# First projection of a hybrid decoder layer: x in 256-column pieces and k-tiles turned two at a time

## The chip, the cores and the metric

The kernel runs on one core of one Trainium2 chip. The metric is the device time of one execution in microseconds (us); the median of three executions stands for a kernel. The other numbers come from one profiled execution of the same program: engine PE is TensorE (PEld its weight load), DVE is VectorE, ACT is ScalarE, POOL is GpSimd, and SP is the engine whose queue issues most of the DMAs. A letter q behind an engine's name means its instruction queue rather than its arithmetic.

## The reference, cut to what matters

One decoder layer over 256 tokens of width 2048, in float32:

```
h    = rms_norm(x, pre_norm_w)                  # x: 256 x 2048
proj = h @ w_in                                 # w_in: 2048 x 12304, cut into q, k, v, z, b, a of branch A
                                                # and q, k, v, z of branch B, and two gates
A    = gated DeltaNet(causal conv + SiLU of q, k, v; beta, g)  -> @ w_branch_a
B    = block-sparse attention(q, k, v)          -> @ w_branch_b
y    = (sigmoid(gate_a) * A + sigmoid(gate_b) * B) @ w_out
out  = x + rms_norm(y, post_norm_w)
```

The change concerns the first stage alone: x is loaded and transposed, and the first 512 of the 1024 key columns of branch A are computed, that is a 256 x 2048 by 2048 x 512 product.

## The kernel before

**Arithmetic.** A float32 operand is cut in two: `hi`, rounded to the matmul's input type, and `lo`, the rest. A product is hi x hi + hi x lo + lo x hi. For one k-tile (128 of the 2048 rows of the weight) the first stage has in SBUF a raw weight tile of 128 x 512 (`rawk`, shown as `rawf_k`), its two parts `hi_k` and `lo_k`, and the matching 128 columns of x, transposed and multiplied by `pre_norm_w`, as `hT[:, k]`: 256 columns of hi and 256 of lo. Four output blocks (`pfirst`, shown as `a_k`) stay in PSUM over all 16 k-tiles. Each k-tile takes four matmuls of `hi_k` with all 512 columns of `hT` and four of `lo_k` with its first 256 columns (`first_products`).

**Where the parts come from.** `turn(c)` transposes k-tiles of x on PE into PSUM (`hTp`; two k-tiles share one PSUM tile, two transposes each). `turned(...)` takes them out: ACT writes the hi half of `hT` (L253, with the norm's weight as scale), then DVE writes the lo half (L256). `first_split(k, 2)` cuts two raw weight tiles at once: ACT casts the hi part (L278, 128x1024), DVE subtracts (L279). `stats(c)` squares and sums 512 columns of x for the norm, one token tile on ACT (L266), the other on DVE (L269).

**Order.** All these instructions are held in the order in which the program writes them on each engine (`pin`); an engine takes its own strictly in that order. The first stage goes by four chunks `c` of 512 columns. SP issues two pieces of x (128 x 512 each) and then four weight tiles for each chunk; the small DMA of `pre_norm_w` (`nrow`) is the first on SP. In chunk c, PE does two k-tiles, then the eight transposes of chunk c + 1, then the other two k-tiles. The weight splits run ahead: when chunk c + 1 is turned (from the second chunk on), the tiles up to 4c + 5 have been split already, and the tiles 4c + 6 to 4c + 9 are split after the chunk's last two k-tiles. The buffers of the weight parts hold three pairs.

**What follows.** After k-tile 15, the sums of squares give `rstd` (a table load and a Sqrt on ACT, L316; small steps on DVE, L315 to L326), PE spreads it (`prr`, L327), and the next projection (`zg`) starts. From there on weights come in larger pieces through `wraw` and `split` (L225, L226).

The rule by which the chunk loop works before:

```
for c in range(NCH):
    first_products(parts[4 * c : 4 * c + 2])
    if c + 1 < NCH:
        turned(turn(c + 1))
    ...
    stats(c)
    first_products(parts[4 * c + 2 : 4 * c + 4])
    for k in (4 * c + 6, 4 * c + 8): ...  parts += first_split(k, 2)
```

Of the kernel before, what the change touches and what calls it, by code (L numbers as in the profile page):

```python
# [15 lines left out]
P = 128  # L16
# [58 lines left out]
def hybrid_layer(  # L75
# [15 lines left out]
    nc = tc.nc  # L91
    B, S, D = x.shape
    NT = S // P
    KT = D // P
# [29 lines left out]
    def acc_tile(name):  # L124
        return acc.tile([P, 512], F32, tag="acc", name=name)

    def aux_tile(name):
        return aux.tile([P, 512], F32, tag="aux", name=name)
# [17 lines left out]
    def mm(*args, **kwargs):  # L146
        return pin(nc.tensor.matmul(*args, **kwargs))  # L147

    def tr(*args):
        return pin(nc.tensor.transpose(*args))  # L150
# [8 lines left out]

    NCH = KT // 4  # L160
    nrow = cst.tile([KT, P], F32, name="nrow")
    nc.sync.dma_start(nrow, pre_norm_w.rearrange("o (k p) -> (o k) p", p=P))
    prow = big.tile([P, P], F32, tag="ga", name="prow")
    xall = big.tile([P, NT, D], F32, tag="u1", name="x")
    xs = [xall[:, t, :] for t in range(NT)]
    rawk = [big.tile([P, KT // 2, 512], F32, tag=f"g{i}", name=f"rawf_k{i}") for i in range(2)]
    for c in range(NCH):
        for t in range(NT):
            cs = slice(c * 512, (c + 1) * 512)
            nc.sync.dma_start(xs[t][:, cs], xf[t * P : (t + 1) * P, cs])  # L170
        for k in range(4 * c, 4 * c + 4):
            nc.sync.dma_start(rawk[k // 8][:, k % 8], w_in[k * P : (k + 1) * P, CK : CK + 512])


# [62 lines left out]
    def turn(c):  # L237

        pts = []
        for k in range(4 * c, 4 * c + 4):  # L240
            if k % 2 == 0:
                pt = aux_tile(f"hTp_{k}")
            pts.append((k, pt[:, k % 2 * S : (k % 2 + 1) * S]))
            for t in range(NT):
                tr(pts[-1][1][:, t * P : (t + 1) * P], xs[t][:, k * P : (k + 1) * P], ident)
        return pts

    def turned(pts):
        for k, pr in pts:
            if k == 1:  # L250
                pin(nc.vector.tensor_scalar_mul(hT[:, k, :S], pr, ncol[:, k : k + 1]))
            else:
                pin(nc.scalar.activation(hT[:, k, :S], pr, AF.Copy, scale=ncol[:, k : k + 1]))  # L253
        for k, pr in pts:
            pin(
                nc.vector.scalar_tensor_tensor(  # L256
                    hT[:, k, S:], pr, ncol[:, k : k + 1], hT[:, k, :S].bitcast(F32), op0=ALU.mult, op1=ALU.subtract
                )
            )

    def stats(c):
        cs = slice(c * 512, (c + 1) * 512)
        for t in range(NT):
            j0 = wk.tile([P, 512], BF16, tag="jy", name=f"jx_{c}_{t}")
            if t == 0:
                pin(nc.scalar.activation(j0, xs[t][:, cs], AF.Square, accum_out=ssx[:, t, c : c + 1]))  # L266
            else:
                pin(
                    nc.vector.scalar_tensor_tensor(  # L269
                        j0, xs[t][:, cs], 1.0, xs[t][:, cs], op0=ALU.mult, op1=ALU.mult, accum_out=ssx[:, t, c : c + 1]  # L270
                    )
                )

    def first_split(k, n):
        hi = wspl.tile([P, 2, 512], F32R, tag="hi", name=f"hi_k0_{k}")
        lo = wspl.tile([P, 2, 512], F32R, tag="lo", name=f"lo_k0_{k}")
        raw = rawk[k // 8][:, k % 8 : k % 8 + n]
        pin(nc.scalar.copy(hi[:, :n], raw))  # L278
        pin(nc.vector.tensor_tensor(lo[:, :n], raw, hi[:, :n].bitcast(F32), op=ALU.subtract))  # L279
        return [(k + i, hi[:, i], lo[:, i]) for i in range(n)]  # L280

    def first_products(parts):
        for k, hi, lo in parts:
            for part in range(2):
                for m in range(4):
                    ms, pt = slice(m * P, (m + 1) * P), pfirst[m]
                    if part == 0:
                        mm(pt, hi[:, ms], hT[:, k, :], start=(k == 0), stop=False)
                    else:
                        mm(pt[:, :S], lo[:, ms], hT[:, k, :S], start=False, stop=(k == KT - 1))  # L290

    pnc = aux_tile("pnc")
    tr(pnc[:, :KT], nrow, ident[:KT, :KT])
    pin(nc.vector.tensor_copy(ncol, pnc[:, :KT]))
    pts = turn(0)
    for i in range(WARM2):
        mm(warm[:, :P], ones, ones, start=True, stop=True)
    turned(pts[:2])
    parts = first_split(0, 1) + first_split(1, 1)
    turned(pts[2:])  # L300
    parts += first_split(2, 2)
    for c in range(NCH):
        first_products(parts[4 * c : 4 * c + 2])
        if c + 1 < NCH:
            turned(turn(c + 1))
        if c == 0:
            parts += first_split(4, 2)
        stats(c)
        first_products(parts[4 * c + 2 : 4 * c + 4])
        for k in (4 * c + 6, 4 * c + 8):  # L310
            if k < KT:
                parts += first_split(k, 2)


    nc.vector.tensor_reduce(rstd, ssx, axis=AX.X, op=ALU.add)  # L315
# [796 lines left out]
    for blk in ORDER:  # L1112
        n, c = blk[:2].rstrip("0123456789"), int(blk[-1])
# [126 lines left out]
    parts = []  # L1240
# [20 lines left out]
    c = 3  # L1261
    pts = [acc_tile(f"a_y{c}_{t}") for t in range(NT)]
# [43 lines left out]
```

## Time and profile before

| what | value |
|---|---|
| median of 3 executions | 778.52 us (778.04 to 779.99) |
| profiled execution, device time | 777.05 us |
| its span, first to last instruction | 775.4 us |
| mean granted TensorE clock | 0.998 |
| PE busy | 763.5 us, 98% of the span |
| PEld / DVE / ACT / POOL busy | 650.2 / 565.2 / 436.1 / 33.5 us |
| DMA | 151.87 MB, mean 196 GB/s |

A line of the timeline gives the start, the time taken, engine, line, operation, what it writes and reads, how many such instructions are merged into it and, in brackets, how long the engine was idle before it and what ended that. A line of the stages' table gives, for each engine, busy time and count, then the granted clock, the share of the DMA engines that was busy and the bandwidth.

### The profile page before, as it was taken

What the parts mean: (1) busy time and instruction counts of PE and PEld (TensorE: products, weight loads), DVE (VectorE), ACT (ScalarE), POOL (GpSimd) and SP (SyncE); (2) the same over time, 40 slices, a digit from 0 to 9 for tenths busy, and PEclk for the clock granted to TensorE, in tenths of its full rate; (3) what the DMA queues carried; (4) which work ended last, traced back from release to release, by engine and by line L of the source; (5) the groups of instructions that cost most, each with busy time, mean ns of one, the idle gap of its engine ahead of it and who ended that gap; (6) DMA issues with size and microseconds to landing.
All of it is one profiled execution on the core that took longest, in us unless ns stands there. A gap on an engine that the chain in (4) does not pass through costs nothing.

```text
span 775.4 us, 10348 instructions
## 1 busy us (share of the span) xinstructions
PE 763.5 (98%) x3923; PEld 650.2 (84%) x3923; DVE 565.2 (73%) x914; ACT 436.1 (56%) x654; POOL 33.5 (4%) x61
## 2 busy tenths in 40 slices
PE   8999999999999999999999999999999999999995
PEld 7898988899888888888889888788888888888884
DVE  5777669885878898775547886686658776888853
ACT  5676666657655664454447475654455544556731
POOL 3000001112000000002001000000000000000000
PEclk9999999999999999999999999999999999999999
DMA  8576675457655556668336556657644956375912
GB/s 302 173 238 214 188 213 170 136 166 220 202 179 202 177 188 196 198 180 217 109 97 217 178 173 216 242 205 251 212 163 152 386 172 212 111 286 193 333 54 109
DMA packets 93656, 151.87 MB, mean 196 GB/s; under 512 B 3237, under 2 KB 46886, under 8 KB 93094
## 3 DMA queue, kind: packets, MB, share of 16 engines
q1 hardware_dynamic: 88902, 134.42, 53.4%
q0 software_dynamic: 4128, 15.74, 6.0%
q10 hardware_dynamic: 576, 1.05, 0.4%
q8 instruction: 31, 0.51, 0.3%
q14 instruction: 19, 0.16, 0.1%
HBM read 148.04 MB, written 3.15 MB: 195 GB/s over the span
## 4 chain that ended last, share of the span: by engine, by line
PE 95%; ACT 2%; DVE 2%; DMA 1%; SPq 0%; issue 0%; DVEq 0%
PE a_gb L147 11%; PE a_y L147 11%; PE a_ga L147 11%; PE a_zg L147 6%; PE a_mq L147 6%; PE a_v L147 6%; PE a_mk L147 6%; PE a_ub L147 6%; PE a_zm L147 6%; PE a_mv L147 5%; PE a_k L147 5%; PE a_ua L147 5%; PE a_q L147 4%; PE sv L147 2%; PE s L147 1%; DMA x<-in_x_dram 1%
## 5 line engine op out<-in xcount | busy, mean ns | idle before, releaser
L147 PE MATMUL a_ga<-hi_ga,hT 128*128 128x512 f32 x256 | 81.9, 393 | 0.0
L147 PE MATMUL a_gb<-hi_gb,hT 128*128 128x512 f32 x256 | 80.2, 390 | 0.0
L226 DVE TENSOR_TENSOR lo_gb<-raw_gb,hi_gb 128x1024 fp32r<-128x1024 f32 x32 | 38.9, 1223 | 25.1 <-ACT hi_gb L225 24.9
L147 PEld LDWEIGHTS a_gb<-hi_gb,hT 128*128 128x128 f32 x256 | 48.0, 188 | 10.6
L147 PEld LDWEIGHTS a_ga<-hi_ga,hT 128*128 128x128 f32 x256 | 48.1, 188 | 10.1
L225 ACT CAST hi_gb<-raw_gb 128x1024 fp32r<-128x1024 f32 x32 | 33.3, 1051 | 35.6 <-PE a_gb L147 26.5
L225 ACT CAST hi_ga<-raw_ga 128x1024 fp32r<-128x1024 f32 x32 | 33.7, 1055 | 34.0 <-PE a_ga L147 16.2
L226 DVE TENSOR_TENSOR lo_ga<-raw_ga,hi_ga 128x1024 fp32r<-128x1024 f32 x32 | 39.0, 1222 | 18.5 <-ACT hi_ga L225 18.3
L147 PE MATMUL a_ga<-lo_ga,hT 128*128 128x512 f32 x128 | 50.0, 391 | 0.1
L147 PE MATMUL a_gb<-lo_gb,hT 128*128 128x512 f32 x128 | 50.0, 391 | 0.0
L147 PE MATMUL a_zg<-hi_zg,hT 128*128 128x348 f32 (+1 forms) x192 | 47.0, 322 | 0.0
L147 PE MATMUL a_mq<-hT,hi_mq 128*128 128x512 f32 x128 | 46.8, 407 | 0.0
L147 PE MATMUL a_mk<-hT,hi_mk 128*128 128x512 f32 x128 | 46.1, 402 | 0.0
L147 PE MATMUL a_y<-hi_y,mT 128*128 128x512 f32 x144 | 46.1, 392 | 0.0
L147 PE MATMUL a_q<-hT,hi_q 128*128 128x512 f32 x128 | 46.0, 399 | 0.0
L147 PE MATMUL a_v<-hT,hi_v 128*128 128x512 f32 x128 | 45.3, 399 | 0.0
L147 PE MATMUL a_ub<-hi_ub,obT 128*128 128x512 f32 x128 | 41.3, 395 | 0.0
L147 PE MATMUL a_k<-hT,hi_k 128*128 128x512 f32 x128 | 40.6, 399 | 0.5 <-ACT hi_k L278 0.5
L147 PE MATMUL a_zm<-hi_zm,hT 128*128 128x512 f32 x128 | 40.5, 392 | 0.0
L147 PE MATMUL a_mv<-hi_mv,hT 128*128 128x512 f32 x128 | 40.1, 391 | 0.0
L147 PE MATMUL a_v<-hT,lo_v 128*128 128x256 f32 x128 | 35.9, 281 | 0.0
L147 PE MATMUL a_q<-hT,lo_q 128*128 128x256 f32 x128 | 35.9, 281 | 0.0
(377 smaller groups left out, 1972.8 us busy)
## 6 DMA issues: line engine op xcount, KB each, us to landing
raw_ga<-in_w_in_dram SPq DMA_DIRECT2D x16, 1024.0 KB, 5.1
raw_gb<-in_w_in_dram SPq DMA_DIRECT2D x16, 1024.0 KB, 5.7
raw_y<-in_w_out_dram SPq DMA_DIRECT2D x15, 1024.0 KB, 5.9
raw_q<-in_w_in_dram SPq DMA_DIRECT2D x8, 1024.0 KB, 5.6
raw_mv<-in_w_in_dram SPq DMA_DIRECT2D x8, 1024.0 KB, 5.1
raw_v<-in_w_in_dram SPq DMA_DIRECT2D x8, 1024.0 KB, 5.7
raw_zm<-in_w_in_dram SPq DMA_DIRECT2D x8, 1024.0 KB, 5.0
raw_mq<-in_w_in_dram SPq DMA_DIRECT2D x8, 1024.0 KB, 5.8
```

The lines of the kernel that those rows point to most:

```text
L147: return pin(nc.tensor.matmul(*args, **kwargs))
L225: nc.scalar.copy(hi, raw)
L226: nc.vector.tensor_tensor(lo, raw, hi.bitcast(F32), op=ALU.subtract)
```

## The change

The DMA of `nrow` moves from SP's queue to ACT's. The loop that loads x and the weights now has eight steps: two pieces of x of 128 x 256, then two weight tiles. `turn(c)` takes two k-tiles (four transposes) in place of four. The main loop has eight steps: k-tile 2c; then the four transposes of the next pair, their way out through ACT and DVE, and the split of that pair's weights; then, in every second step, the statistics; then k-tile 2c + 1. The weight splits therefore no longer run two pairs ahead: those of pair c + 1 are written after the transposes of pair c + 1.

```diff
-    nc.sync.dma_start(nrow, pre_norm_w.rearrange("o (k p) -> (o k) p", p=P))
+    nc.scalar.dma_start(nrow, pre_norm_w.rearrange("o (k p) -> (o k) p", p=P))
...
-    for c in range(NCH):
-        for t in range(NT):
-            cs = slice(c * 512, (c + 1) * 512)
+    for c in range(KT // 2):
+
+        for t in range(NT):
+            cs = slice(c * 256, (c + 1) * 256)
             nc.sync.dma_start(xs[t][:, cs], xf[t * P : (t + 1) * P, cs])
-        for k in range(4 * c, 4 * c + 4):
+        for k in range(2 * c, 2 * c + 2):
             nc.sync.dma_start(rawk[k // 8][:, k % 8], w_in[k * P : (k + 1) * P, CK : CK + 512])
...
     def turn(c):
 
         pts = []
-        for k in range(4 * c, 4 * c + 4):
+        for k in range(2 * c, 2 * c + 2):
...
-    turned(pts[:2])
+    turned(pts)
     parts = first_split(0, 1) + first_split(1, 1)
-    turned(pts[2:])
-    parts += first_split(2, 2)
-    for c in range(NCH):
-        first_products(parts[4 * c : 4 * c + 2])
-        if c + 1 < NCH:
+    for c in range(KT // 2):
+        first_products(parts[2 * c : 2 * c + 1])
+        if 2 * c + 2 < KT:
             turned(turn(c + 1))
-        if c == 0:
-            parts += first_split(4, 2)
-        stats(c)
-        first_products(parts[4 * c + 2 : 4 * c + 4])
-        for k in (4 * c + 6, 4 * c + 8):
-            if k < KT:
-                parts += first_split(k, 2)
+            parts += first_split(2 * c + 2, 2)
+        if c % 2 == 1:
+            stats(c // 2)
+        first_products(parts[2 * c + 1 : 2 * c + 2])
```

## The prediction

> **What bounds the kernel now.** I read the page's busy times and its chain first, then a table of stages, then the waits of PE, then the timeline of the first 34 us, where the change lies.
>
> ```profile
> span 775.4 us, 10348 instructions
> ...
> PE 763.5 (98%) x3923; PEld 650.2 (84%) x3923; DVE 565.2 (73%) x914; ACT 436.1 (56%) x654; POOL 33.5 (4%) x61
> ...
> PE 95%; ACT 2%; DVE 2%; DMA 1%; SPq 0%; issue 0%; DVEq 0%
> ```
>
> PE is busy for 98% of the span and carries 95% of the chain. What the change does must therefore show as time in which PE stands, and time that PE loses early comes back only if PE later waits for something else.
>
> ```profile
> 0.00:8.20 8.20, 5.13 (x27) 4.43 (x28) 1.49 (x7) 2.98 (x6) 7.25 (x20) 1.00 0.64 202
> 8.20:12.20 4.00, 3.85 (x23) 3.22 (x24) 3.39 (x6) 1.94 (x5) 0.27 (x1) 1.00 1.02 351
> 12.20:33.75 21.55, 21.55 (x131) 18.94 (x130) 17.03 (x34) 16.11 (x31) 0.00 (x0) 1.00 0.73 254
> 33.75:120.00 86.25, 86.17 (x485) 77.90 (x485) 63.54 (x131) 57.44 (x96) 1.23 (x2) 1.00 0.65 200
> ```
>
> Columns: the stretch, its length, busy time of PE, PEld, DVE, ACT, POOL with counts, clock, DMA share, GB/s. From 12.20 us to the end of the first stage PE is busy in all of 21.55 us, and in the next 86.25 us it stands for 0.08. So there are two things to win in the old first stage, the start before 8.20 us and what PE lost between 8.20 and 12.20, and there is nothing behind it that would absorb a loss.
>
> ```profile
> PE hTp L150 <- DMA x<-in_x_dram: 1.5, 2, 0.9
> ```
>
> ```profile
> 4.89 0.14 PEld L150 LDWEIGHTS hTp<-ident,x 128*128 128x128 f32 x1 [0.74 <-DMA x<-in_x_dram]
> 6.11 0.75 PEld L150 LDWEIGHTS hTp<-ident,x 128*128 128x128 f32 x7 [1.07 <-DMA x<-in_x_dram]
> 8.20 0.76 PEld L147 LDWEIGHTS a_k<-hT,hi_k 128*128 128x128 f32 x4 [0.62 <-ACT hi_k L278]
> 9.12 0.54 PEld L147 LDWEIGHTS a_k<-hT,lo_k 128*128 128x128 f32 x4 [0.17 <-DVE lo_k L279]
> 9.59 0.77 PEld L147 LDWEIGHTS a_k<-hT,hi_k 128*128 128x128 f32 x4
> 11.50 0.75 PEld L150 LDWEIGHTS hTp<-ident,x 128*128 128x128 f32 x7 [0.36 <-DMA x<-in_x_dram]
> ```
>
> The first transposes wait for x at 4.89 and 6.11, the first product starts at 8.20, and one later transpose waits 0.36 us for x. That is the whole visible target. I count by weight loads, which are issued just ahead of their matmuls.
>
> **Part 1: the start.** Issue times and landings bound it.
>
> ```profile
> 0.81 0.39 SPq L162 DMA_DIRECT2D nrow<-in_pre_norm_w_dram  x1
> 1.25 0.88 SPq L170 DMA_DIRECT2D x<-in_x_dram  x2
> 2.18 1.85 SPq L172 DMA_DIRECT2D rawf_k<-in_w_in_dram  x4
> ...
> 770.26 1.66 ACTq L1231 DMA_DIRECT2D out_dram<-yw  x2
> ```
>
> With `nrow` gone from SP, the first piece of x goes out at 0.81 in place of 1.25, 0.44 earlier, and the second at about 1.25. Both together now hold 256 KB, as much as the first piece alone held before, which had landed by 4.89. If bytes count, the second piece lands 0.44 ahead of that, at 4.4; if each DMA costs the same whatever its size, it lands 0.44 ahead of the old second piece, 5.7. I take 4.85, nearer to the bytes, since the issue of the second piece is no earlier than the old first one's was. From the transposes released at 6.11 to the first product at 8.20 were 2.09 us, through ACT's and DVE's work on k-tiles 0 and 1, which the changed program orders in the same way. So the first product starts at 4.85 + 2.09 = 6.94 (6.5 to 7.8): **1.26 us gained**, bounds 0.4 to 1.7. Moving `nrow` I cost at nothing: two DMA issues on ACT took 1.66 us, so one takes at most about 0.9, and ACT has no work that PE needs before its first taking-out of a transpose (below, at 6.70). If that cover were gone it would cost those 0.9. The wait of 0.36 us at 11.50 goes, since the next x pieces now stand behind two weight tiles and not four.
>
> The Trainium skill's page "DMA: Bandwidth & Descriptors", section "Rules for kernel authors", speaks against smaller pieces: it asks for 1 MiB per DMA for full bandwidth, and puts a fixed 2.0 us on each transfer beside its bytes. By its fit, an estimate, 128 KB would take 2.3 us and 256 KB 2.6, so that halving saves 0.3 us and the start would gain 0.7 in all. The trace agrees in part: 256 KB pieces already ran at 351 GB/s in the second row of the stages.
>
> **Part 2: the period of a pair.** The changed program's instruction order reads, on ACT, for each pair: two hi halves of `hT`, then the cast of that same pair's weights, then in every second pair the statistics. On DVE: two lo halves, then the weights' lo part. On PE: k-tile 2c, four transposes, k-tile 2c + 1, k-tile 2c + 2. The cast therefore stands behind two instructions that wait for PE's transposes, although its data are long there, and k-tile 2c + 2 must wait for it with only one k-tile in between as cover.
>
> ```profile
> 12.09 1.57 ACT L253 ACTIVATE hT<-hTp,ncol 128x256 fp32r<-128x256 f32 x4 [1.99 <-PE hTp L150]
> 13.53 1.06 ACT L278 CAST hi_k<-rawf_k 128x1024 fp32r<-128x1024 f32 x1
> 13.61 0.77 PEld L147 LDWEIGHTS a_k<-hT,hi_k 128*128 128x128 f32 x4
> 14.47 0.66 ACT L266 ACTIVATE jx<-x 128x512 bf16<-128x512 f32 x1
> 15.01 0.77 PEld L147 LDWEIGHTS a_k<-hT,hi_k 128*128 128x128 f32 x4
> 17.04 1.05 ACT L278 CAST hi_k<-rawf_k 128x1024 fp32r<-128x1024 f32 x1 [0.88 <-DMA rawf_k<-in_w_in_dram]
> 17.82 0.90 PEld L150 LDWEIGHTS hTp<-ident,x 128*128 128x128 f32 x8
> 18.12 1.23 DVE L279 TENSOR_TENSOR lo_k<-rawf_k,hi_k 128x1024 fp32r<-128x1024 f32 x1 [0.52 <-ACT hi_k L278]
> 18.55 1.57 ACT L253 ACTIVATE hT<-hTp,ncol 128x256 fp32r<-128x256 f32 x4 [0.46 <-PE hTp L150]
> 18.68 0.77 PEld L147 LDWEIGHTS a_k<-hT,hi_k 128*128 128x128 f32 x4
> 24.30 0.90 PEld L150 LDWEIGHTS hTp<-ident,x 128*128 128x128 f32 x8
> ```
>
> Let T be the first transpose of a turn. ACT starts on `hT` 18.55 - 17.82 = 0.73 later (there it waited for the first four transposes, which is all of a turn now). Four `hT` instructions held the cast back by 13.53 - 12.09 = 1.44, so two take 0.72: cast at T + 1.45. From a cast to the DVE instruction that it releases are 18.12 - 17.04 = 1.08: lo part from T + 2.53, and 1.23 long, to T + 3.76. The matmuls with `hi_k` start at about T + 2.55 and are issued by 3.5; those with `lo_k` wait until 3.81 (0.05, as at 9.12, behind a DVE instruction) and take 9.59 - 9.12 = 0.47. The next turn starts at **T + 4.28**. DVE's two lo halves of `hT` fit in before T + 2.4, so they add nothing.
>
> PE's own work for a pair is half of 24.30 - 17.82 = 6.48, that is 3.24 (two k-tiles of 15.01 - 13.61 = 1.40 and four transposes of half of 18.68 - 17.82 = 0.86). PE thus stands 1.04 us in every pair. I allow 0.25 us each way for waits that the rows show only in their own surroundings. The statistics stand behind the cast on ACT and behind the lo part on DVE and end before the next turn needs either.
>
> **Part 3: the end of the stage.** The last statistics now come after the last cast, and the norm's small chain stands behind them and behind two casts of the next projection.
>
> ```profile
> 28.03 0.64 ACT L266 ACTIVATE jx<-x 128x512 bf16<-128x512 f32 x1
> 28.65 0.77 ACT L225 CAST hi_zg<-raw_zg 128x688 fp32r<-128x688 f32 x1
> 30.60 0.77 ACT L225 CAST hi_zg<-raw_zg 128x688 fp32r<-128x688 f32 x1 [1.17 <-PE a_k L147]
> 31.38 1.28 ACT L316 ACT_TABLE_LOAD   x1
> 32.68 0.29 ACT L316 ACTIVATE rstd<-rstd,epst 128x2 f32<-128x2 f32 x1
> 33.75 0.52 PEld L147 LDWEIGHTS prr<-dg,ones 128*128 128x128 f32 x4
> ```
>
> Counted from the last turn T7: cast at 1.45, statistics 0.94 later (14.47 - 13.53) at 2.39, first zg cast 0.62 later at 3.01, the second at 3.75 (its buffer is free by then), table load at 4.5, Sqrt 1.30 later at 5.8, and from Sqrt to `prr` 33.75 - 32.68 = 1.07: T7 + 6.87. PE itself is through with k-tile 15 at T7 + 4.28 + 1.40 = 5.68. So PE would stand another 1.19 us for the norm's chain, which before ended just in time; between nothing and 1.2 I take it whole, as the order on ACT is fixed.
>
> **The sum.** First product 6.94; first turn T1 = 6.94 + (9.59 - 8.20 = 1.39) = 8.33; T7 = 8.33 + 6 x 4.28 = 34.0; `prr` at 34.0 + 6.87 = 40.9, against 33.75 before: **+7.1 us**. In parts: start -1.26, wait for x -0.36, seven pairs +7.3, four more transposes inside the stage +0.43, norm chain +1.19, rounding -0.2. Behind the stage PE is dense, so the shift stays. Span 775.4 + 7.1 = 782.5; the profiled execution's 777.05 (1.65 around its span) would be 784.2; it lies 1.5 under the median of the runs, so the median is 778.5 + 7.1 = **785.6**.
>
> **Queues.** SP issues eight DMAs more, some 0.44 us each, 3.5 us in all, less `nrow`. Behind them stand the small constants and the first zg weights, which are needed only after T7.
>
> **Rivals.**
>
> *Enough throughput hides it (not slower).* In the dense stretch ACT was busy 16.11 and DVE 17.03 of 21.55 us; per pair ACT has some 2.0 us of work and DVE 2.3, both under PE's 3.24. Were the pairs to run at PE's pace, the start and the x wait alone would count: 778.5 - 1.26 - 0.36 = 776.9, with the best start 776.5. For it speak the busy shares. Against it speaks the order: the chain from a turn to the next goes once through PE, ACT and DVE in a row, so latency and not share decides. It decides for no change once the period is below about 3.6, and 0.7 us would have to vanish from rows quoted above. Chance 0.07, mostly as no change.
>
> *The DMAs become the bound (slower still).*
>
> ```profile
> DMA to landing us min/median/max: 5.1/5.4/6.9
> ```
>
> That is for the weight tiles. The issues wait for the eighth DMA before them, so eight are in flight, now two pairs with 1.5 MB in place of 2 MB. At 5.4 us to land, a pair comes every 2.7 us, at the worst 6.9 every 3.45: both below 4.28. A period of 5.0, landing in 10 us, would add 0.7 x 7 = 5: 790.6. Chance 0.04.
>
> *The clock falls (slower still).* With two short stands in each pair PE could lose its clock.
>
> ```profile
> 1.12 2.93 PE L147 MATMUL warm<-ones 128*128 128x128 f32 x12 [1.12 <-DVE epst L181]
> 6.93 0.83 PE L147 MATMUL warm<-ones 128*128 128x128 f32 x6
> ```
>
> At the very start twelve warm-up matmuls took 0.24 us each, later ones 0.14. At that slower pace the hi matmuls of a tile take 1.6 us, the lo ones 0.8, and the period grows to about 5.3: +7 more, 793. But before 8.20 PE was busy only 5.13 of 8.20 us and its later matmuls were fast already. Chance 0.03. The Trainium skill's page "TensorE: Matmul & The Clock Gate", section "A second HAM failure mode: psum-queue depth-cycling", has this case: frequent micro-idles between groups of matmuls can make the gate swing. The trace's start, with gaps of 0.4 to 1.1 us at a clock of 1.00, does not show it.
>
> **The numbers.** Forecast 0.86, rivals 0.07, 0.04, 0.03. In the forecast: start 0.9 late or 0.4 early, period 0.25 each way (1.75 over seven), norm chain down to nothing (-1.2), run to run about 0.7. Together that gives 782.3 to 789.0, which holds about 8 in 10. About 0.3% (2.3 us) is what a measurement of this kernel can tell from no change: faster 0.02, same 0.06, slower 0.92.
>
> **What would show it.** Right: first product near 6.9; PEld lines of `hTp` x4 every 4.3 us; behind each, `a_k<-hT,hi_k` idle some 0.7 us for ACT hi_k, and `lo_k` some 0.3 for DVE; `prr` near 41 after some 1.2 us of waiting. Wrong: turns every 3.3 us, or PE's waits named after DMA x or rawf_k, or a clock under 1.00 in the stage.

## The result and the profile after

| | before | changed |
|---|---|---|
| median, us | 778.28 (777.05 to 779.99, 4 runs) | 784.31 (784.05 to 784.51, 4 runs) |
| profiled execution, us | 777.05 | 784.05 |
| its span, us | 775.4 | 782.2 |
| `prr` issued at, us | 33.75 | 41.00 |

The changed kernel takes 1.0075 of the time of before, with a 95% interval of 1.0058 to 1.0091: 6.0 us by the medians, 7.0 by the two profiled executions.

The page of the changed kernel, its busy times and the engines of its chain:

```profile
span 782.2 us, 10359 instructions
...
PE 766.9 (98%) x3923; PEld 650.4 (83%) x3923; DVE 567.0 (72%) x914; ACT 435.9 (56%) x654; POOL 33.8 (4%) x61
...
PE 92%; ACT 3%; DVE 3%; DMA 1%; SPq 1%; issue 0%; DVEq 0%; ACTq 0%
```

PE's share of the chain has gone from 95% to 92%; ACT and DVE together have gone from 4% to 6%. The page alone would not tell where. The stages do, cut at the first product, the first and the last turn, and `prr`:

```profile
0.00:6.71 6.71, 4.72 (x23) 4.27 (x23) 1.48 (x7) 2.97 (x5) 5.82 (x19) 1.00 0.66 200
6.71:8.34 1.63, 1.60 (x8) 1.16 (x9) 1.63 (x3) 0.00 (x1) 1.56 (x2) 1.00 0.94 286
8.34:34.16 25.82, 22.64 (x123) 17.19 (x121) 15.38 (x25) 12.50 (x24) 0.47 (x1) 1.00 0.75 258
34.16:41.00 6.84, 5.43 (x31) 4.14 (x30) 5.14 (x16) 6.07 (x11) 0.00 (x0) 1.00 0.00 1
41.00:127.30 86.30, 86.21 (x485) 77.97 (x486) 63.65 (x131) 56.96 (x95) 1.23 (x2) 1.00 0.66 200
```

In the six periods from 8.34 to 34.16 (4.30 us each) PE is not busy for 3.2 us, and part of what counts as busy are matmuls drawn out while the next weights are missing (by the weight loads below, PE stands 0.68 and 0.50 us in one period). ACT works 12.50 and DVE 15.38 of 25.82 us: neither is full. Behind 41.00 PE is as dense as it was. The waits of PE name who holds it:

```profile
PE a_k L147 <- ACT hi_k L279: 4.2, 8, 0.9
...
PE prr L147 <- DVE dg L322: 0.9, 1, 0.9
```

No wait for a DMA is among them. One period in order of time shows the trip of a pair through PE, ACT and DVE and back to PE:

```profile
16.93 0.47 PEld L150 LDWEIGHTS hTp<-ident,x 128*128 128x128 f32 x4
17.37 0.76 PEld L147 LDWEIGHTS a_k<-hT,hi_k 128*128 128x128 f32 x4
17.68 0.84 ACT L254 ACTIVATE hT<-hTp,ncol 128x256 fp32r<-128x256 f32 x2 [1.91 <-PE hTp L150]
18.18 0.65 PEld L147 LDWEIGHTS a_k<-hT,lo_k 128*128 128x128 f32 x4
18.40 1.05 ACT L279 CAST hi_k<-rawf_k 128x1024 fp32r<-128x1024 f32 x1
18.55 0.88 DVE L257 SCALAR_TENSOR_TENSOR hT<-hTp,ncol,hT 128x256 fp32r<-128x256 f32 x2 [1.53 <-ACT hT L254]
19.48 1.23 DVE L280 TENSOR_TENSOR lo_k<-rawf_k,hi_k 128x1024 fp32r<-128x1024 f32 x1
19.50 0.76 PEld L147 LDWEIGHTS a_k<-hT,hi_k 128*128 128x128 f32 x4 [0.68 <-ACT hi_k L279]
20.77 0.54 PEld L147 LDWEIGHTS a_k<-hT,lo_k 128*128 128x128 f32 x4 [0.50 <-DVE lo_k L280]
21.25 0.46 PEld L150 LDWEIGHTS hTp<-ident,x 128*128 128x128 f32 x4
```

Read it as one chain: the turn at 16.93 lets ACT begin at 17.68; the cast stands behind the two `hT` instructions and begins at 18.40; at 19.50 PE gets its hi weights after 0.68 us of standing, at 20.77 its lo weights after another 0.50; the next turn can only follow that, at 21.25. ACT had been idle for 1.91 us before 17.68, with the raw weights of the cast already there (their DMAs were issued by 9.4 us, and no weight tile took more than 5.0 us to land).

### The profile page after: what moved, and what is told of

Same layout as the page of the kernel before. It is cut to its first block, busy times and chain, and to the rows that moved or that the text cites. A ratio compares the mean times of both kernels' runs of the same rounds, so it can differ in the third digit from the quotient of the medians.

```text
span 782.2 us, 10359 instructions
## 1 busy us (share of the span) xinstructions
PE 766.9 (98%) x3923; PEld 650.4 (83%) x3923; DVE 567.0 (72%) x914; ACT 435.9 (56%) x654; POOL 33.8 (4%) x61
## 3 DMA queue, kind: packets, MB, share of 16 engines
q10 hardware_dynamic: 608, 1.06, 0.4%
## 4 chain that ended last, share of the span: by engine, by line
PE 92%; ACT 3%; DVE 3%; DMA 1%; SPq 1%; issue 0%; DVEq 0%; ACTq 0%
PE a_gb L147 11%; PE a_y L147 11%; PE a_ga L147 11%; PE a_zg L147 6%; PE a_mq L147 6%; PE a_mk L147 6%; PE a_v L147 6%; PE a_ub L147 6%; PE a_zm L147 6%; PE a_mv L147 5%; PE a_ua L147 5%; PE a_q L147 4%; PE a_k L147 4%; PE sv L147 2%; PE s L147 1%; DMA rawf_k<-in_w_in_dram 1%
```

## The experiments

My theory was that of the prediction: the order on ACT and DVE makes one trip through three engines the period. The rivals were the smaller loads, turns of four transposes as such, and the clock. Times of the first four experiments stand against 778.08 us of before (19 runs on that chip), of the other four against 777.67 (26 runs on theirs).

**Split first.**

```diff
-            turned(turn(c + 1))
             parts += first_split(2 * c + 2, 2)
+            turned(turn(c + 1))
```

> The changed kernel with two lines swapped: the weights of the next pair are split (ACT cast, DVE subtraction) before the next pair of x is turned, so the cast no longer stands behind two ACT instructions that wait for PE. Theory (the order on ACT and DVE makes the period of 4.30 us): then only the way out of PSUM is left between a turn and its use, 1.61 to DVE's first lo half, 0.48 for it and 0.05 to PE, 2.15 us after the turn, where PE is free after 1.83; period 3.56, prr near 37, and the time 4.1 us under the changed kernel's 784.3, about 780.2. PE should no longer wait for ACT hi_k except at the second pair, whose weights land near 9.0. Rival (the smaller pieces of x, or four transposes per turn by themselves, cost the time): period stays 4.3, time 784 within 1.

Measured: 779.35 us, 1.0018 of before (1.0008 to 1.0027). Two lines in another order give back most of the loss: 5.0 us by the medians, 4.4 by the two ratios. Its timeline:

```profile
8.89 1.05 ACT L279 CAST hi_k<-rawf_k 128x1024 fp32r<-128x1024 f32 x1 [1.57 <-DMA rawf_k<-in_w_in_dram]
...
15.20 0.76 PEld L147 LDWEIGHTS a_k<-hT,hi_k 128*128 128x128 f32 x4 [0.26 <-DVE hT L257]
16.60 0.46 PEld L150 LDWEIGHTS hTp<-ident,x 128*128 128x128 f32 x4
...
20.18 0.46 PEld L150 LDWEIGHTS hTp<-ident,x 128*128 128x128 f32 x4
...
36.06 0.52 PEld L147 LDWEIGHTS prr<-dg,ones 128*128 128x128 f32 x4 [0.23 <-PE a_k L147]
```

The period is 3.58 between these two turns (3.56 forecast), the wait before the hi weights 0.26, now for DVE's lo half of `hT`, and the one before the lo weights is gone. The loads and the turns of four are unchanged, so neither makes the 4.30. Only the first period is longer, 4.70 us (8.34 to 13.04): there the cast, now first in line, waits for its weights, and the two `hT` instructions wait behind it. That the norm's chain costs less too (0.23 in place of 1.08 us) had not been counted.

**The loads alone**, with the old order of the work:

```diff
-    nc.sync.dma_start(nrow, ...)
+    nc.scalar.dma_start(nrow, ...)
...
-            cs = slice(c * 512, (c + 1) * 512)     # in a loop of four chunks
+            cs = slice(c * 256, (c + 1) * 256)     # in a loop of eight pieces
```

> The loads of the change alone (pieces of 256 columns, nrow on ACT's queue), with the old order of the work: eight transposes at a time, splits ahead. Theory: the old order needs 512 columns before its first product and 1024 before its third; the second chunk's last piece lands near 11.84 in the changed trace where it landed at 11.46, and from there PE is dense, so the stage ends 0.3 to 0.4 us later: 778.6, no change that can be told. Rival A (the loads are what costs): 782 or more, with PE waiting for DMA. Rival B (the head start of 1.5 us belongs to the loads alone): 776.8.

Measured: 778.26 us, 1.000 of before (0.9991 to 1.0010). The loads alone cost and gain nothing that can be told. How the profiled execution came to that is not what I had expected. First the two waits on its timeline, then its stages, cut where the granted clock changed:

```profile
6.50 0.14 PEld L150 LDWEIGHTS hTp<-ident,x 128*128 128x128 f32 x1 [1.82 <-DMA x<-in_x_dram]
7.38 0.31 PEld L150 LDWEIGHTS hTp<-ident,x 128*128 128x128 f32 x3 [0.74 <-DMA x<-in_x_dram]
```

```profile
4.36:7.77 3.41, 1.27 (x9) 0.84 (x9) 2.44 (x6) 1.71 (x3) 3.21 (x4) 1.00 0.97 324
7.77:11.18 3.41, 3.41 (x14) 3.02 (x13) 3.29 (x5) 1.88 (x3) 1.05 (x1) 0.50 1.02 363
11.18:35.10 23.92, 23.92 (x147) 21.14 (x146) 17.24 (x35) 16.11 (x31) 0.00 (x0) 1.00 0.72 238
```

The old order needs 512 columns before its first product, and with weights between the pieces the second 256 come at 6.50 and 7.38. PE is busy in 1.27 of 3.41 us, and for the next 3.41 us the granted clock is half. `prr` is at 35.11, 1.36 us behind the profiled execution of before. So the old order loses the head start: it belongs to loads and turns together.

**The turns alone**, with the old loads:

```diff
-    nc.scalar.dma_start(nrow, ...)
+    nc.sync.dma_start(nrow, ...)
...
-            cs = slice(c * 256, (c + 1) * 256)     # in a loop of eight pieces
+            cs = slice(c * 512, (c + 1) * 512)     # in a loop of four chunks
```

> The order of the change alone (two k-tiles turned at a time, splits behind them), with the old loads (pieces of 512 columns, four weight tiles behind them, nrow first on SP). Theory: period 4.30 as in the changed kernel, first product at about 8.2 in place of 6.71, so 1.3 to 1.5 us over the changed kernel: 785.7, prr near 42.4. Rival (the smaller loads make the period): period near 3.3, time 779 or less.

Measured: 787.17 us, 1.0115 (1.0100 to 1.0130): 2.9 us more than the changed kernel, where 1.4 were expected. From its timeline:

```profile
8.52 2.05 PE L147 MATMUL a_k<-hT,hi_k 128*128 128x512 f32 x4 [0.29 <-ACT hi_k L278]
...
10.82 0.46 PEld L150 LDWEIGHTS hTp<-ident,x 128*128 128x128 f32 x4
15.12 0.46 PEld L150 LDWEIGHTS hTp<-ident,x 128*128 128x128 f32 x4
...
43.46 0.52 PEld L147 LDWEIGHTS prr<-dg,ones 128*128 128x128 f32 x4 [1.09 <-PE a_k L147]
```

The period is 4.30 with the large loads too, so it belongs to the order alone. The first product comes 1.8 us later than in the changed kernel, and its four hi matmuls take 2.05 us where they took 1.16 there: PE had not reached its full pace. The trace's record of the clock begins with its first full stretch, at 10.55 us in this run and at 4.90 in the changed kernel; ahead of that the stages' tables print 1.00 without a record. So the first turn is 2.5 us later than the changed kernel's 8.34, and `prr` too; 1 us more than I had expected, all of it ahead of the first turn.

**Statistics earlier.**

```diff
+        if c == 6:
+            stats(3)
         if 2 * c + 2 < KT:
             turned(turn(c + 1))
             parts += first_split(2 * c + 2, 2)
-        if c % 2 == 1:
+        if c % 2 == 1 and c < 7:
```

> The changed kernel with the last statistics (columns 1536 to 2047 of x) one step earlier, ahead of the last turn. The scheduler then puts the table load and the Sqrt ahead of the zg casts on ACT. Theory: PE's wait of 1.08 us before prr goes whole, prr near 39.9, and the time is 783.2; the period stays 4.30. Rival (the wait before prr is PE's own tail and only shows there): prr stays at 41.0 and the time at 784.3.

Measured: 783.75 us, 1.0076 (1.0061 to 1.0091). The time cannot tell 1 us apart here; the trace can:

```profile
36.67 1.28 ACT L314 ACT_TABLE_LOAD   x1
...
38.95 0.88 DVE L227 TENSOR_TENSOR lo_zg<-raw_zg,hi_zg 128x688 fp32r<-128x688 f32 x1 [0.49 <-ACT hi_zg L226]
...
40.28 0.52 PEld L147 LDWEIGHTS prr<-dg,ones 128*128 128x128 f32 x4 [0.38 <-PE a_k L147]
```

The wait fell from 1.08 to 0.38 us, not to nothing: on DVE a subtraction for zg, which waits for ACT, now stands ahead of the last steps of the norm.

**All a pair earlier.**

```diff
+        if c == 0:
+            turned(turn(1))
+            parts += first_split(2, 1) + first_split(3, 1)
+        if c == 5:
+            stats(3)
         first_products(parts[2 * c + 1 : 2 * c + 2])
+        if 2 * c + 4 < KT:
+            turned(turn(c + 2))
+            parts += first_split(2 * c + 4, 2)
+        if c in (1, 3, 4):
+            stats((1, 3, 4).index(c))
```

(the change's own turn, split and statistics in the loop are gone)

> The changed kernel's loads and pairs, but each pair of x is turned, taken out and split one pair earlier (the turn of pair c + 2 and its splits follow k-tile 2c + 1), and the last statistics come at step 5. Theory (the period of 4.30 us is the latency of one trip through PE, ACT and DVE, for which one k-tile of 1.40 us is too little cover and a whole pair of 3.24 us is enough): the turns come every 3.24 to 3.3 us, PE no longer waits for ACT or DVE after the third k-tile, prr near 32.5. With the changed kernel's own distance from prr to its time (784.3 - 41.0 = 743.3) that is 775.8, 2.3 under the 778.1 of before. Rival (four transposes at a time or the smaller loads cost by themselves): period 3.6 or more, 778 or more.

Measured: 775.87 us (775.45 to 776.22, 10 runs), 0.9977 of before (0.9968 to 0.9986). It beats both kernels. A line of its stages, then its timeline:

```profile
10.18:32.47 22.29, 22.29 (x139) 19.73 (x137) 18.34 (x37) 17.14 (x33) 0.00 (x0) 1.00 0.79 266
```

```profile
13.41 0.46 PEld L150 LDWEIGHTS hTp<-ident,x 128*128 128x128 f32 x4
...
16.65 0.46 PEld L150 LDWEIGHTS hTp<-ident,x 128*128 128x128 f32 x4
...
32.47 0.52 PEld L147 LDWEIGHTS prr<-dg,ones 128*128 128x128 f32 x4
```

The period is 3.24, PE's own work for a pair, and PE is busy throughout, with the change's loads and its turns of four. This run also moves the last statistics ahead, so the wait before `prr` goes too: the 8.53 us between its `prr` and the changed kernel's are, within 0.05, seven periods at 1.06 less and the 1.08 of that wait. So small turns and small loads are not bad in themselves; with a whole pair to cover the trip the kernel is 1.8 us faster than before by the medians. In the profiled executions `prr` comes 1.28 us earlier than before's; the rest of the 1.8 has the spread of before's runs in it, which the next run is about.

**Before, kept at work.**

```diff
+    for i in range(4):
+        mm(warm[:, :P], ones, ones, start=True, stop=True)
     pts = turn(0)
```

> The kernel before with four more warm-up matmuls, put on PE between the turn of the norm's weights and the first x, where PE stands from 4.3 to 6.1 us. Theory: before's profiled execution (full clock from 4.67 us, prr at 33.75, 777.05) was a good one, and its usual 778.1 holds about 1.0 us in which the first products ran at half clock; with PE kept at work the clock is full for the first products more often, and the median falls to 777.1 or a little over, with less spread. Rival (the spread of before has another cause, at the end or in the loads): 778.1 with the same spread of 2.6 us.

Measured: 777.00 us (776.61 to 777.67, 11 runs), 0.9992 (0.9984 to 1.0001), against 776.47 to 779.01 of before. The spread went from 2.5 to 1.1 us, as expected, and the middle half of the runs from 0.7 to 0.3; the median's fall of 0.7 us has an interval that reaches just past no change. Its first products took 1.17 us for four hi matmuls (8.43 to 9.60), but so did those of before's profiled execution, whose 777.05 lies low among its runs, and `prr` comes at 34.10, not ahead of its 33.75: the gain is not visible in the two traces. That part of before's usual time is a slow start of PE is thus supported, not settled. For it speaks the turns-alone run, which has before's loads and such a start in its trace, 0.9 us at the first hi matmuls, and the loads-alone run, in which PE also stands for x: it spreads over 2.4 us in 10 runs, where the split-first run and the one with all a pair earlier spread over 1.0 and 0.8. Against it speaks that one of the four runs of statistics earlier, where PE does not stand for x either, is 1.3 us above the other three. And some of the spread lies outside the span: before's device time is 1.66 to 2.82 us over its span in those 26 runs, 1.67 to 1.85 in these 11.

**GpSimd later.**

```diff
+    held_tv = big.tile([P, 16, 64], F32, tag="tv", name="held_tv")
+    nc.vector.memset(held_tv[:, 0, 0:4], 0.0)
...
     nc.vector.tensor_scalar_mul(nrstd, rstd, -1.0)
+    nc.vector.tensor_scalar_mul(held_tv[:, 0, 0:2], rstd, -1.0)
```

> The changed kernel with GpSimd's work on the tile tv (a memset and four selections, 2.7 to 8.8 us) held back until rstd is known. Theory (DVE's first two subtractions, 0.89 and 1.62 us in place of 0.68, were slowed by GpSimd working at the same time): both take 0.68, the first lo matmuls start at 7.65 in place of 7.85, the stage ends 0.2 earlier, 784.1. The selections then meet DVE's work behind prr, at a time where DVE has room. Rival (they were slowed by the loads, which were landing in the same tile at that time): 0.89 and 1.62 stay.

Measured: 786.48 us, 1.0114 (1.0100 to 1.0127): 2.2 us more than the changed kernel by the medians, 3.0 by the ratios. The mechanism shows, and a cost that I had not seen. First the changed kernel, then this one:

```profile
3.71 5.10 POOL L626 TENSOR_SCALAR_AFFINE_SELECT tv<-tv 32x1024 f32<-32x1024 f32 x4
...
6.91 2.44 DVE L280 TENSOR_TENSOR lo_k<-rawf_k,hi_k 128x512 fp32r<-128x512 f32 x2
```

```profile
7.04 1.28 DVE L283 TENSOR_TENSOR lo_k<-rawf_k,hi_k 128x512 fp32r<-128x512 f32 x2
...
40.58 1.18 DVE L326 TENSOR_SCALAR dg<-ident,rstd 128x128 f32<-128x128 f32 x2
40.66 0.95 POOL L628 MEMSET tv<- 128x1024 f32 x1 [37.88 <-DVE held_tv L319]
...
41.80 0.52 PEld L147 LDWEIGHTS prr<-dg,ones 128*128 128x128 f32 x4 [1.98 <-issue]
```

Without GpSimd beside them DVE's first two subtractions take 1.28 us together in place of 2.44, though the first lo matmuls start at 7.78 us, 0.07 earlier than in the changed kernel and not 0.2, as this execution's first hi weights came at 6.85 in place of 6.71. The loads are the changed kernel's, so GpSimd it was, and not the landing of the loads. But the same work now falls on `dg`, two instructions of the norm's chain: 1.18 us in place of 0.47 in the changed kernel. PE stands 1.98 us before `prr`, and then a stage at half clock follows:

```profile
43.52:46.94 3.42, 3.42 (x14) 3.42 (x13) 1.50 (x5) 0.70 (x2) 3.22 (x4) 0.50 0.07 20
```

`prr` comes 0.80 us later than in the changed kernel, and half pace for 3.42 us costs another 1.7: an estimate of 2.5 for the 2.2 to 3.0 measured. My claim that DVE has room there was wrong, since `dg` is on the path.

**All together**: all a pair earlier, GpSimd held back, and `WARM2 = 5` in place of 3.

> The kernel of the first run of this group (all a pair earlier) with GpSimd's tile held back as in the third and two more warm-up matmuls before the first product (five in place of three). Theory: 0.2 us less than that first run and a clock that does not fall before the first product: 775.6. Rival (the warm-ups delay the first product, 6.7 us, because they end near 6.5 at full clock and later at half): 0.3 to 0.5 more than the first run.

Measured: 776.65 us, 0.9986 (0.9977 to 0.9995): 0.8 more than without the two additions. The rival had the sign, with another cause, visible at the end of the stage:

```profile
32.04 1.18 DVE L331 TENSOR_SCALAR dg<-ident,rstd 128x128 f32<-128x128 f32 x2
32.12 0.95 POOL L633 MEMSET tv<- 128x1024 f32 x1 [29.35 <-DVE held_tv L324]
33.27 0.52 PEld L147 LDWEIGHTS prr<-dg,ones 128*128 128x128 f32 x4 [0.92 <-PE a_k L147]
```

As in the run before, `dg` meets GpSimd, and PE waits 0.92 us for it, where the version without the additions does not wait. The first product came at 6.81, against 6.85 without the additions, and not later.

## Why the prediction was right, and where it was off

**Start.** The second piece of x was estimated at 4.85 us; PE's transposes did not wait for x at all:

```profile
4.20 0.71 PEld L150 LDWEIGHTS hTp<-ident,x 128*128 128x128 f32 x4
...
6.71 0.76 PEld L147 LDWEIGHTS a_k<-hT,hi_k 128*128 128x128 f32 x4 [1.06 <-ACT hi_k L279]
```

They follow the turn of the norm's weights at 3.98 at once. So the second piece landed at about the lower bound, 4.4, or ahead of it. From there to the first product I had 2.09 us and it was 2.51. The difference lies ahead of the first taking-out by ACT, here in before and in the changed kernel:

```profile
6.70 0.47 ACT L253 ACTIVATE hT<-hTp,ncol 128x256 fp32r<-128x256 f32 x1 [4.41 <-PE hTp L150]
```

```profile
5.21 0.47 ACT L254 ACTIVATE hT<-hTp,ncol 128x256 fp32r<-128x256 f32 x1 [2.48 <-PE hTp L150]
```

From there both take 1.50 us to the first product. Up to there it was 0.59 from 6.11 in before and is 1.01 from 4.20 now; a later turn takes 0.73 (8.34 to 9.07). So 0.14 of the 0.42 comes from the row I used, in which one of the four transposes had been done at 4.89 already, and 0.28 from the slower pace of these early transposes (0.71 us for four weight loads, later 0.46), which lie ahead of the 4.90 us where the clock's record begins. The two misses cancel in part, which is luck: 6.71 in place of 6.94, a gain of 1.49 in place of 1.26. How much of it the move of `nrow` brings and how much the smaller pieces, no run separates. The estimate that the prediction worked out from the Trainium skill's page "DMA: Bandwidth & Descriptors", a gain of 0.7, fell short too; the page gives that fit, in its section "Anatomy of one DMA — SWDGE (gpsimd) path", for DMAs issued by GpSimd, and here SP issues them.

**Period.** 4.28 was forecast, 4.30 measured, with ACT, cast, DVE and PE in the places the sum gave them. The split-first run shows that the cast's place is what made it, the run with the turns alone that the loads do not, and the run with all a pair earlier that neither the pieces nor the small turns do. This step was right for its reason.

**End.** `prr` at 40.9 was forecast, 41.00 measured; the wait 1.19 forecast, 1.08 measured. The statistics-early run shows that most of it is the order around the statistics: 0.70 of the 1.08 goes with them.

**From the trace to the median.** Here lies the miss, 785.6 against 784.31. The sum for the profiled execution, 784.2, met 784.05, in part by luck: `prr` came 7.25 us later and not 7.1, and 0.4 went behind it. I then added 1.5 us because before's profiled execution lay that far under its median. The changed kernel has no such distance: its runs lie within 784.05 to 784.51. Over five of the profiled executions, the distance from `prr` to the device time hardly varies: 743.3 before, 743.1 changed, 743.5 and 743.0 in the split-first and the all-earlier runs, 743.6 in the warmed kernel. What spreads before's runs is thus more likely ahead of `prr`, though of before itself only one execution has a trace, and some of the spread is outside the span. PE's slow start is the candidate that the warmed kernel supports.

**Rivals.** Throughput did not hide the loss: with the same instructions for a pair on ACT and DVE, 4.30 or 3.24 us came from the order alone. The DMAs were not the bound. The clock did not fall in the stage itself (1.00 from 8.34 to 41.00), so stands of 0.68 and 0.50 us in each period did not lower it; it fell in other runs, after longer ones. That the shift stays behind `prr` held but for 0.4 us: of the 7.25 at `prr` 6.8 are left at the end of the span. They go while PE is dense in both kernels, in the last products of `a_v` (from 203 to 222 us in the changed kernel), where six weight loads take 1.04 us against 1.06 in before; why is open.

## What to carry to other kernels

Where one engine is dense and the others are half idle, ask of every moved step which instruction it now stands behind, and add up the trip through all engines against the work that covers it. Here one k-tile, 1.40 us of PE's work, was too little cover, and a period of 3.24 became 4.30: a loss that the busy shares of ACT and DVE, well under full, do not show. A look-ahead is cheap to keep: two lines in another order took back 4 to 5 us, and one pair more of distance turned a loss of 6 us into a gain of 1.8. Take the distance from a profiled execution to the median from several runs, and not over to another kernel.

## What the runs showed of the hardware that was not expected

- The granted clock can halve without a long stand. With the loads alone, after 3.41 us in which PE was busy for 1.27, the longest stand 1.82, it was 0.50 for the next 3.41 us; in the GpSimd-later run 1.69 us of work, the longest stand 1.98, did the same. Before had 1.99 us of work in the 3.41 us with which its record of the clock begins, and kept 1.00. Here are these stretches of before and of the GpSimd-later run:

```profile
4.67:8.08 3.41, 1.99 (x14) 1.61 (x14) 0.88 (x3) 1.38 (x3) 3.21 (x4) 1.00 0.97 334
```

```profile
40.11:43.52 3.41, 1.69 (x11) 1.52 (x12) 3.30 (x11) 1.76 (x6) 2.79 (x2) 1.00 0.69 192
```

  The Trainium skill's page "TensorE: Matmul & The Clock Gate", section "Why this matters for your kernels", warns of idle gaps over about 3 us. The length of the slow stretch is that of the window in the page's section "What's actually happening", but shorter stands sufficed here.
- DVE's subtraction of two SBUF tiles and GpSimd's selection slow each other: 2.44 us in place of 1.28 for two subtractions. The Trainium skill's page "SBUF — State Buffer", section "SBUF: two separate sides", describes a port pair that DVE and GpSimd hold in turn, which agrees; here GpSimd's last selection also grew, to 1.48 us from 1.14, its four taking 5.10 us where before's took 4.76:

```profile
3.71 4.76 POOL L630 TENSOR_SCALAR_AFFINE_SELECT tv<-tv 32x1024 f32<-32x1024 f32 x4
```
